# Attention stacks on SyncE's queue as plain float32, the first head's straight from SBUF; layer 1's last modulations beside its attention

## The chip, the cores and the metric

The kernel runs on one core of one Trainium2 chip. A core has a matrix engine (TensorE, PE in the profile), a vector engine (VectorE, DVE), an activation engine (ScalarE, ACT), GpSimd (POOL) and SyncE (SP), which only issues DMAs. Each engine works through its own list of instructions in order and waits at semaphores for the others. DMAs are issued by SP and by POOL here; they move data between DRAM, the large memory, and SBUF, the on-chip one of 128 partitions. Matmuls write to PSUM. The metric is the device time of one execution in microseconds.

## The reference, cut to what matters

Two layers work on 512 latent and 256 context tokens of 1024 features. In each layer a normalized and modulated input is projected, four mixers run side by side (an S5 state-space scan, a gated recurrence, differential attention, gated linear attention), each is projected and multiplied with a gate, and their sum is projected into the residual; then a feed-forward net with a small convolution follows. The second layer computes latent tokens only at its output.

```python
# modulation: six chunks of 1024 per layer from the conditioning vector
m = jax.nn.silu(cond) @ w[:, :n_chunks * D_MODEL] + b[:n_chunks * D_MODEL]
...
# differential attention: 4 heads, 2 components of 32 features each
s = jnp.einsum('bhcqd,bhckd->bhcqk', q, k).astype(F32) * (DA_HEAD ** -0.5)
p = jax.nn.softmax(s, axis=-1)
w = p[:, :, 0] - lam * p[:, :, 1]
return jnp.einsum('bhqk,bhkv->bhqv', w.astype(v.dtype), v)
```

The sixth chunk of the modulation is the gate with which the feed-forward net's result goes into the residual.

## The kernel before, in words

[...] To keep precision each operand is split into a high part and the rest (`hi`, `lo`), and a product is three matmuls: hi x hi, lo x hi, hi x lo. Weights come from DRAM by `load_raw` (line 183, on SP's queue) into a ring of four buffers `wraw`; ScalarE casts the high part (`whi`, line 193), VectorE subtracts (`wlo`, line 194), and the matmuls of `proj` (line 220) use both. Features lie on the partitions, tokens along the free dimension.

The attention's scores are made another way. Each of the eight (head, component) groups has 32 features, a quarter of the partitions. So the four products hi/lo by hi/lo of a group are stacked along the partitions into one matmul of 128: the queries' tile `dstq` holds rows hi, hi, lo, lo and the keys' tile `dstk` hi, lo, hi, lo, 32 partitions each. `da_prep` (line 845) normalizes and rotates queries and keys of two heads and splits them into `dhi` and `dlo`, and writes both into a DRAM buffer `dstk{layer}{half}{q or k}` (line 863). `da_stack` (line 867) reads the tiles of one head back from there, with each row block read twice: four DMAs for queries (line 876) and two for keys (line 879). All of these DMAs are issued by GpSimd; the tiles `dstq` and `dstk` have the type float32r, the DRAM buffer float32.

`da_mix` prepares the first two heads, stacks head 0, prepares the other two, and then runs through the heads: at the start of head h it asks for the stacks of head h+1, then makes scores (lines 925 to 928), the softmax and the products with the values of each tile of 128 queries. Tiles `dstq` and `dstk` come from a pool of ten buffers, shared with others, so that the stacks of a head wait for those of the head before last to be free.

The order of the instructions on each engine is written out by a planner ahead of the run. It takes the instructions by priority (the program's order, and `first()` and `mixer()` put the mixers ahead) as soon as its own estimate of the times says that their inputs and buffers are there. The first scores are tied behind the last matmul of a fixed number of merges (`lead`, `DA_LEAD`). Beside the attention, PE works on gates and branch projections (`merge_branch`), in layer 1 also on six gates made early.

The modulations are made by `ada` (matmuls of line 282, closing ones of line 269): a pair of column blocks at a time, with two loads of 512 KB on SP's queue whose `wraw` buffers the matmuls read directly. `LAST` are the last four pairs, the sixth chunk. They run in the feed-forward net of their own layer: two steps ahead of it (`FILL2`, in the gap of the normalization), the others between its blocks (`side`).

Of the kernel before, what the change touches and what calls it, by code (L numbers as in the profile page):

```python
# [22 lines left out]
T = NLAT + NCTX  # L23
DEPTH = 2
# [50 lines left out]
def f32(ap):  # L75
    return ap.bitcast(F32)
# [3 lines left out]
def backbone(ctx, tc, xT, cT, w_ada, w_in, w_v, w_ga, w_branch, w_out, w_up, w_down, vec,  # L80
             s5_b, s5_c, s5_d, w_glu, lru_w, gla_wa2, consts, masks, rope, cmask, out, dbg=None):
    nc = tc.nc
# [21 lines left out]
    def H(name, shape=None, dt=F32):  # L104
        return gp_.tile(shape or [P, 512], dt, tag="h", name=name, bufs=6)
# [41 lines left out]
    def V(l, name):  # L147
        o, n = VOFF[name]
        return vt[l][:, o:o + n]
# [9 lines left out]
    for l in range(DEPTH):  # L159
        t = cpool.tile([P, 3, 4], F32, name=f"lru_s{l}")  # L160
# [142 lines left out]
    FIRST = range(KT)  # L303
    REST = range(KT, 20)
    LAST = range(20, 24)
# [113 lines left out]
    for l in range(DEPTH):  # L419
# [3 lines left out]
            k=dp.tile([2, P, 240], F32, name=f"s5k{l}"),  # L423
# [421 lines left out]
    def da_prep(l, i, qk, sg, qgs, rp):  # L845

        v = nc.vector
        stk = []
        for which, z, s_, gain in (("q", qk[0], sg, qgs), ("k", qk[1], [LAT, CTX], V(l, 'k_g'))):
            n = s_[-1][1]  # L850
            r = group_rstd(z, C('bo32'), DA_HEAD, s_, "d" + which)
            v.tensor_scalar_mul(z[:, :n], z[:, :n], gain)
            sw = G("dsw")
            v.stream_shuffle(sw[:, :NLAT], z[:, :NLAT], [j ^ 8 for j in range(32)])
            v.tensor_mul(z[:, :NLAT], z[:, :NLAT], rp[0])
            v.tensor_mul(sw[:, :NLAT], sw[:, :NLAT], rp[1])
            v.tensor_add(z[:, :NLAT], z[:, :NLAT], sw[:, :NLAT])
            v.tensor_mul(z[:, :n], z[:, :n], r[:, :n])
            hi, lo = G("dhi", dt=F32R), G("dlo", dt=F32R)
            split(z, hi, lo, 0, n)  # L860
            dd = dp.tile([4, 2, 32, T], F32, name=f"dstk{l}{i}{which}")
            for p_, t_ in enumerate((hi, lo)):
                nc.gpsimd.dma_start(dd[:, p_, :, :n], f32(t_[:, :n]))
            stk.append(dd)
        return stk

    def da_stack(stk, hh, sg):
        res = []
        for dd, n, which in ((stk[0], sg[-1][1], "q"), (stk[1], T, "k")):
            ts = []  # L870
            for c in range(2):
                g = hh * 2 + c
                t = Z("dst" + which, dt=F32R)
                if which == "q":
                    for p_ in range(2):
                        nc.gpsimd.dma_start(t[64 * p_:64 * p_ + 64, :n],
                                            dd[g, p_][:, :n].unsqueeze(0).broadcast_to([2, 32, n]))
                else:
                    nc.gpsimd.dma_start(t[:, :n],
                                        dd[g].rearrange("h r n -> (h r) n")[:, :n].unsqueeze(0).broadcast_to([2, 64, n]))  # L880
                ts.append(t)
            res.append(ts)
        return res

    def da_mix(l, qks, vt_, lat_only):
        v = nc.vector
        e = NLAT if lat_only else T
        sg = [LAT] if lat_only else [LAT, CTX]
# [20 lines left out]
        yield  # L909
        res = []  # L910
        stks = [da_prep(l, 0, qks[0], sg, qgs, rp)]
        st = da_stack(stks[0], 0, sg)
        stks.append(da_prep(l, 1, qks[1], sg, qgs, rp))
        o = None
        lead = yield
# [69 lines left out]
        for hd in range(4):  # L985
            cur = st
            if hd < 3:
                st = da_stack(stks[(hd + 1) // 2], (hd + 1) % 2, sg)
# [188 lines left out]
    def drain(gen):  # L1177
        while True:
            try:
                next(gen)  # L1180
            except StopIteration as s:
                return s.value
# [11 lines left out]
    def chain(*gens):  # L1194
        for g in gens:
            yield from g

    def zipgen(main, fill, n):
        for _ in main:
            for _ in range(n):  # L1200
                next(fill, None)
            yield
# [18 lines left out]
    def gate(l, b, m, h, sg, t):  # L1221
        w = load_split(w_in[l, 18 + b * 8 + m])
        proj("ps_g", w, h, sg, lambda ps, a, b: nc.scalar.activation(t[:, a:b], ps, AF.Tanh, scale=0.5))
        return t

    def merge_branch(l, b, h, y, acc, sg, first, gates=()):

        v = nc.vector
        wb = None
        for m in range(KT):  # L1230
            if m % 4 == 0:
                wb = load_split(w_branch[l, b, m // 4], nk=2, cols=512)
            if m < len(gates):
                t = gates[m]
            else:
                t = gate(l, b, m, h, sg, gp_.tile([P, T], F32, tag="gate", name="gate", bufs=2))
            if first:
                acc.append(X("acc"))

            def use(ps, a, b):  # L1240
                dst = acc[m] if first else t
                v.scalar_tensor_tensor(dst[:, a:b], t[:, a:b], 1.0, ps, op0=ALU.add, op1=ALU.mult)  # L1242
                if not first:
                    v.tensor_add(acc[m][:, a:b], acc[m][:, a:b], t[:, a:b])
            proj("ps_p", wb, y, sg, use, c0=(m % 4) * P)
            yield
# [63 lines left out]
    for l in range(DEPTH):  # L1310
        lat_only = l == DEPTH - 1
        sg = [LAT] if lat_only else sg_all
        if l == 0:
            with first() if NF else nullcontext():
                h = norm_mod(l, x, V(l, 'norm1'), 0, 1, [(0, T)], (marks[M0], marks[M1]))
        else:
            with first():
                h = norm_mod(l, x, V(l, 'norm1'), 0, 1, sg_all)
        for k in range(KT):
            dump(f"h{l}_{k}", f32(h[k][0]))  # L1320
        if l == 0:
            xd = xT
        else:
            xd = dp.tile([KT, P, T], F32, name="x_spill")
            for k in range(KT):
                nc.gpsimd.dma_start(xd[k][:, :NLAT], x[k][:, :NLAT])
        rest = ada(l, REST) if l == 0 else iter(())
        acc = []
        if l == 0:
            with tc.high_priority(offset=-PREP_LAST):  # L1330
                for _ in range(PREP_EARLY):
                    next(prep)
        li = lru_in(l, h, sg_all, sg)
        if l == 0:
            with tc.high_priority(offset=-PREP_LAST), tc.issue_after(li[2]):
                drain(prep)
        yl = mixer(lru_mix(l, *li[:2], lat_only))
        ud = s5_u(l, h, sg_all)
        gi = gla_in(l, h, sg_all, sg)
        yg = mixer(gla_mix(l, *gi, lat_only))  # L1340
        ys = mixer(s5_mix(l, ud, lat_only))
        drain(zipgen(merge_branch(l, 1, h, yl, acc, sg, True), rest, 1))
        qk0 = da_qk(l, h, 0, sg_all, sg)
        dv = proj_tok(l, 0, h, "dv")
        qk1 = da_qk(l, h, 1, sg_all, sg)
        dm = da_mix(l, (qk0, qk1), dv, lat_only)
        with first():
            next(dm)
            next(dm)
        mb = merge_branch(l, 3, h, yg, acc, sg, False)  # L1350
        for _ in range(DA_LEAD[l]):
            next(mb)
            next(rest, None)
        yd_ = mixer(sent(dm, lastp[0]))
        drain(zipgen(mb, rest, 1))
        drain(zipgen(merge_branch(l, 0, h, ys, acc, sg, False), rest, 1))
        early = [gate(l, 2, m, h, sg, H("gate")) for m in range(EARLY if lat_only else 0)]
        drain(zipgen(merge_branch(l, 2, h, yd_, acc, sg, False, early), rest, 1))
        drain(rest)
        for nm, yy in (("yb", yl), ("yd", yg), ("yc", yd_), ("ya", ys)):  # L1360
            for i in range(2):
                dump(f"{nm}{l}_{i}", f32(yy[i][0]))
        e = sg[-1][1]
        x = [X(f"x{k}") for k in range(KT)]
        with after():
            for k in range(KT):
                nc.sync.dma_start(x[k][:, :e], xd[k][:, :e])
        parts = [(0, 256), (256, NLAT)] if lat_only else sg_all
        out_proj(l, acc, x, sg, parts)
        for k in range(KT):  # L1370
            dump(f"xm{l}_{k}", x[k])
        with first():
            h = norm_mod(l, x, V(l, 'norm2'), 3, 4, parts)
        nxt = chain(ada(l, LAST), *([ada(l + 1, FIRST), ada(l + 1, REST)] if l + 1 < DEPTH else []))
        for _ in range(FILL2):
            next(nxt)
        if l + 1 < DEPTH:
            with tc.high_priority(offset=-PREP_LAST):
                drain(s5_prep(l + 1))
        def side():  # L1380
            for _ in range(2):
                next(nxt, None)
        ffn(l, h, x, sg, side)
        drain(nxt)
        for k in range(KT):
            dump(f"xo{l}_{k}", x[k])
# [128 lines left out]
```

## Time and profile before

| | |
|---|---|
| median of 3 runs | 2375.47 us (2369.54 to 2381.79) |
| the profiled execution | 2370.35 us, its span 2368.6 us |
| PE busy | 2262.0 us, 96% of the span |
| VectorE, ScalarE busy | 1327.7 us (56%), 914.5 us (39%) |
| mean granted clock of TensorE | 0.976 |
| DMA on SP's queue | 222.13 MB |
| DMA on GpSimd's queue | 33.70 MB |

A share of busy time is an average over the whole span. Where PE stands still is seen in the list of waits and in the chain of work that ended last, and what happens at such a place in the timeline of the engines around it. [...]

### The profile page before, as it was taken

What the parts mean: (1) busy time and instruction counts of PE and PEld (TensorE: products, weight loads), DVE (VectorE), ACT (ScalarE), POOL (GpSimd) and SP (SyncE); (2) the same over time, 40 slices, a digit from 0 to 9 for tenths busy, and PEclk for the clock granted to TensorE, in tenths of its full rate; (3) what the DMA queues carried; (4) which work ended last, traced back from release to release, by engine and by line L of the source; (5) the groups of instructions that cost most, each with busy time, mean ns of one, the idle gap of its engine ahead of it and who ended that gap; (6) DMA issues with size and microseconds to landing.
All of it is one profiled execution on the core that took longest, in us unless ns stands there. A gap on an engine that the chain in (4) does not pass through costs nothing. (4 is left out here: it accounts for less than half of the span.)

```text
span 2368.6 us, 34594 instructions
## 1 busy us (share of the span) xinstructions
PE 2262.0 (96%) x13848; PEld 1895.3 (80%) x13848; DVE 1327.7 (56%) x2831; ACT 914.5 (39%) x1428; POOL 101.3 (4%) x164
## 2 busy tenths in 40 slices
PE   5999999699999999999999999999979899999999
PEld 3788788588888788888888887878858688888887
DVE  7886663576674585343334347465557655444444
ACT  6735133445432333132121226633355643323332
POOL 0010000200000010000000000000021000000000
PEclk8999999799999999999999999999989999999999
DMA  7243234554223244233232332224454333333332
GB/s 268 89 140 124 72 114 130 124 129 107 83 98 116 72 128 134 89 111 102 91 101 87 116 121 74 83 87 120 124 130 116 76 101 104 120 111 89 90 111 75
DMA packets 128176, 258.04 MB, mean 109 GB/s; under 512 B 52816, under 2 KB 61072, under 8 KB 128016
## 3 DMA queue, kind: packets, MB, share of 16 engines
q1 hardware_dynamic: 85136, 222.13, 29.4%
q0 software_dynamic: 42880, 33.70, 6.1%
q8 instruction: 109, 1.79, 0.3%
q14 instruction: 51, 0.42, 0.1%
HBM read 230.78 MB, written 24.87 MB: 108 GB/s over the span
## 5 line engine op out<-in xcount | busy, mean ns | idle before, releaser
L194 DVE TENSOR_TENSOR wlo<-wraw,whi 128x1024 fp32r<-128x1024 f32 (+2 forms) x284 | 325.7, 1148 | 327.9 <-ACT whi L193 308.2
L193 ACT CAST whi<-wraw 128x1024 fp32r<-128x1024 f32 (+2 forms) x284 | 280.6, 989 | 579.6 <-PE ps_fd L220 211.6
L220 PE MATMUL ps_g<-hi,whi 128*128 128x512 f32 (+1 forms) x768 | 278.8, 363 | 2.8 <-DVE gate L1242 2.8
L220 PE MATMUL ps_g<-hi,wlo 128*128 128x512 f32 (+1 forms) x768 | 276.5, 360 | 0.0
L220 PE MATMUL ps_g<-lo,whi 128*128 128x512 f32 (+1 forms) x768 | 275.9, 359 | 0.0
L220 PE MATMUL ps_fg<-hi,whi 128*128 128x512 f32 (+1 forms) x544 | 195.0, 360 | 8.0 <-ACT hi L366 7.4
L220 PE MATMUL ps_fg<-hi,wlo 128*128 128x512 f32 (+1 forms) x544 | 191.6, 353 | 0.0
L220 PE MATMUL ps_fg<-lo,whi 128*128 128x512 f32 (+1 forms) x544 | 188.4, 354 | 0.0
L220 PE MATMUL ps_fa<-hi,whi 128*128 128x512 f32 (+1 forms) x528 | 187.5, 355 | 0.0
L220 PE MATMUL ps_fa<-lo,whi 128*128 128x512 f32 (+1 forms) x528 | 187.3, 355 | 0.0
L220 PE MATMUL ps_fd<-uhi,whi 128*128 128x512 f32 (+1 forms) x528 | 187.2, 355 | 0.0
L220 PE MATMUL ps_fd<-ulo,whi 128*128 128x512 f32 (+1 forms) x528 | 187.0, 355 | 0.0
L220 PE MATMUL ps_fa<-hi,wlo 128*128 128x512 f32 (+1 forms) x528 | 186.9, 354 | 0.0
L220 PE MATMUL ps_fd<-uhi,wlo 128*128 128x512 f32 (+1 forms) x528 | 186.0, 354 | 0.0
L220 PEld LDWEIGHTS ps_g<-hi,whi 128*128 128x128 f32 x768 | 145.9, 190 | 29.6 <-issue 5.5
L220 PEld LDWEIGHTS ps_g<-hi,wlo 128*128 128x128 f32 x768 | 145.6, 190 | 23.2 <-issue 2.4
L220 PEld LDWEIGHTS ps_g<-lo,whi 128*128 128x128 f32 x768 | 146.0, 190 | 21.9 <-issue 1.6
L1292 DVE SCALAR_TENSOR_TENSOR x<-ps_fd,mod,x 128x512 f32<-128x512 f32 (+1 forms) x96 | 63.2, 661 | 149.6 <-PE ps_fd L220 149.4
L220 PEld LDWEIGHTS ps_fg<-hi,whi 128*128 128x128 f32 x544 | 104.5, 192 | 31.5 <-ACT hi L366 8.9
L220 PEld LDWEIGHTS ps_fg<-hi,wlo 128*128 128x128 f32 x544 | 105.1, 193 | 13.9 <-issue 1.0
L1285 DVE TENSOR_TENSOR fy<-ps_fa,fy 128x512 f32<-128x512 f32 x66 | 39.8, 603 | 132.3 <-PE ps_fa L220 132.3
L220 PEld LDWEIGHTS ps_fd<-uhi,whi 128*128 128x128 f32 x528 | 99.8, 189 | 15.7 <-DVE fy L1285 1.6
(471 smaller groups left out, 4743.9 us busy)
## 6 DMA issues: line engine op xcount, KB each, us to landing
wraw<-in_w_ada_dram SPq DMA_DIRECT2D x96, 512.0 KB, 3.5
wraw<-in_w_in_dram SPq DMA_DIRECT2D x92, 512.0 KB, 3.9
wraw<-in_w_up_dram SPq DMA_DIRECT2D x88, 512.0 KB, 3.5
wraw<-in_w_down_dram SPq DMA_DIRECT2D x32, 384.0 KB, 3.2
wraw<-in_w_down_dram SPq DMA_DIRECT2D x32, 320.0 KB, 3.0
wraw<-in_w_branch_dram SPq DMA_DIRECT2D x16, 512.0 KB, 5.0
wraw<-in_w_out_dram SPq DMA_DIRECT2D x16, 512.0 KB, 3.6
x<-in_xT_dram SPq DMA_DIRECT2D x16, 384.0 KB, 4.7
```

The source lines that it names most:

```text
L193: nc.scalar.copy(hi, raw)
L194: nc.vector.tensor_sub(lo, raw, f32(hi))
L220: lastp[0] = nc.tensor.matmul(ps[:, c - a:d - a], wt[:, k, c0:c0 + P], act[k][x_][:, c:d], start=i == 0, stop=i == 3 * n - 1).ins
L1285: proj("ps_fa", wa, h, sg, lambda ps, a, b: v.tensor_mul(y[:, a:b], ps, y[:, a:b]), late=f < LATE2)
L1292: v.scalar_tensor_tensor(x[m][:, a:b], ps, mods[l][:, 5 * KT + m, i:i + 1], x[m][:, a:b], op0=ALU.mult, op1=ALU.add)
```

## The change

The attention's writes to DRAM and reads from there are issued by SP, and the tiles are seen as plain float32, so that source and destination have one type. The stacks of head 0 no longer go through DRAM: each of their row blocks is copied from `dhi` or `dlo` in SBUF to the tile in SBUF, four copies of 32 partitions a tile, sixteen in all. The writes to DRAM of the first two heads stay, as head 1 is read from there. In layer 1 the last four pairs of the modulation are asked for in the program ahead of the early gates, beside the attention; nothing is left there to be made in the feed-forward net of layer 1.

```diff
             for p_, t_ in enumerate((hi, lo)):
-                nc.gpsimd.dma_start(dd[:, p_, :, :n], f32(t_[:, :n]))
-            stk.append(dd)
+                nc.sync.dma_start(dd[:, p_, :, :n], f32(t_[:, :n]))
+            stk.append((dd, hi, lo))
         return stk
 
-    def da_stack(stk, hh, sg):
+    def da_stack(stk, hh, sg, direct=False):
+
         res = []
-        for dd, n, which in ((stk[0], sg[-1][1], "q"), (stk[1], T, "k")):
+        for (dd, hi, lo), n, which in ((stk[0], sg[-1][1], "q"), (stk[1], T, "k")):
             ts = []
             for c in range(2):
                 g = hh * 2 + c
                 t = Z("dst" + which, dt=F32R)
-                if which == "q":
+                if direct:
+                    for r in range(4):
+                        p_ = r // 2 if which == "q" else r % 2
+                        nc.sync.dma_start(f32(t[32 * r:32 * r + 32, :n]), f32((hi, lo)[p_][32 * g:32 * g + 32, :n]))
+                elif which == "q":
                     for p_ in range(2):
-                        nc.gpsimd.dma_start(t[64 * p_:64 * p_ + 64, :n],
-                                            dd[g, p_][:, :n].unsqueeze(0).broadcast_to([2, 32, n]))
+                        nc.sync.dma_start(f32(t[64 * p_:64 * p_ + 64, :n]),
+                                          dd[g, p_][:, :n].unsqueeze(0).broadcast_to([2, 32, n]))
                 else:
-                    nc.gpsimd.dma_start(t[:, :n],
-                                        dd[g].rearrange("h r n -> (h r) n")[:, :n].unsqueeze(0).broadcast_to([2, 64, n]))
+                    nc.sync.dma_start(f32(t[:, :n]),
+                                      dd[g].rearrange("h r n -> (h r) n")[:, :n].unsqueeze(0).broadcast_to([2, 64, n]))
                 ts.append(t)
...
         stks = [da_prep(l, 0, qks[0], sg, qgs, rp)]
-        st = da_stack(stks[0], 0, sg)
+        st = da_stack(stks[0], 0, sg, True)
...
         drain(zipgen(merge_branch(l, 0, h, ys, acc, sg, False), rest, 1))
+        if lat_only:
+            drain(ada(l, LAST))
         early = [gate(l, 2, m, h, sg, H("gate")) for m in range(EARLY if lat_only else 0)]
...
-        nxt = chain(ada(l, LAST), *([ada(l + 1, FIRST), ada(l + 1, REST)] if l + 1 < DEPTH else []))
+        nxt = iter(()) if lat_only else chain(ada(l, LAST), ada(l + 1, FIRST), ada(l + 1, REST))
         for _ in range(FILL2):
-            next(nxt)
+            next(nxt, None)
```

## Rows read from the trace of the kernel before

**Rows 1.** The page: busy us, share of the span and instructions.
```profile
PE 2262.0 (96%) x13848; PEld 1895.3 (80%) x13848; DVE 1327.7 (56%) x2831; ACT 914.5 (39%) x1428; POOL 101.3 (4%) x164
```
**Rows 2.** Waits of PE: who waited for whom, us in total, times, longest.
```profile
PE ps_s L925 <- DMA dstq<-dstk00q: 21.0, 1, 21.0
...
PE ps_s L925 <- DMA dstq<-dstk10q: 14.0, 1, 14.0
```
**Rows 3.** Timeline of PE, first scores of both layers: start, us, what [idle before].
```profile
457.46 0.77 PE L925 MATMUL ps_s<-dstk,dstq 128*128 128x512 f32 x1 [20.99 <-DMA dstq<-dstk00q]
...
1762.58 0.77 PE L925 MATMUL ps_s<-dstk,dstq 128*128 128x512 f32 x1 [14.05 <-DMA dstq<-dstk10q]
```
**Rows 4.** Windows: us, busy us by engine, granted clock, DMA share, GB/s.
```profile
460.00:470.00 10.00, 10.00 (x52) 7.29 (x45) 8.16 (x25) 6.02 (x8) 1.53 (x2) 0.87 0.80 219
...
1765.00:1770.00 5.00, 5.00 (x19) 3.76 (x18) 4.41 (x6) 0.84 (x2) 0.67 (x1) 0.86 0.61 107
```
**Rows 5.** Timeline of VectorE: the low part of the first keys, both layers.
```profile
427.26 0.95 DVE L200 TENSOR_TENSOR dlo<-dzk,dhi 128x768 fp32r<-128x768 f32 x1
...
1734.48 0.95 DVE L200 TENSOR_TENSOR dlo<-dzk,dhi 128x768 fp32r<-128x768 f32 x1
```
**Rows 6.** Timeline of POOL: DMA issues of the stacks.
```profile
431.74 0.72 POOL L863 DMA_DIRECT2D dstk00k<-dhi  x1
...
443.89 1.62 POOL L879 DMA_DIRECT2D dstk<-dstk00k  x2 [10.73 <-DMA dstk00k<-dlo]
...
504.20 2.63 POOL L876 DMA_DIRECT2D dstq<-dstk01q  x4 [31.15 <-PE ps_ada L269]
...
550.56 2.68 POOL L876 DMA_DIRECT2D dstq<-dstk01q  x4 [34.26 <-PE ps_s L932]
...
1801.52 2.63 POOL L876 DMA_DIRECT2D dstq<-dstk11q  x4 [20.71 <-PE ps_s L928]
...
1833.90 2.60 POOL L876 DMA_DIRECT2D dstq<-dstk11q  x4 [24.32 <-PE ps_s L928]
```
**Rows 7.** Timeline of SP: one weight load near layer 1's first scores.
```profile
1749.44 0.33 SPq L183 DMA_DIRECT2D wraw<-in_w_in_dram  x1
```
**Rows 8.** DMA issues: line's tiles, queue, count, KB each, median us to landing.
```profile
s5ph<-cph POOLq DMA_DIRECT2D x4, 384.0 KB, 3.1
...
s5u<-us SPq DMA_DIRECT2D x4, 384.0 KB, 2.4
...
dstk00q<-dhi POOLq DMA_DIRECT2D x1, 384.0 KB, 8.9
dstk00q<-dlo POOLq DMA_DIRECT2D x1, 384.0 KB, 12.8
```
**Rows 9.** Tiles dstq (first line) and dstk (second): their DMAs.
```profile
DMA to landing us min/median/max: 5.3/9.4/15.1
...
DMA to landing us min/median/max: 11.5/14.8/18.2
```
**Rows 10.** Chain that ended last, start of layer 1's feed-forward net: start, us, what.
```profile
1988.89 5.12 DMA wraw<-in_w_up_dram
...
2002.40 1.00 PE ps_ada L282 x16
...
2005.72 0.34 PE ps_ada L269 x4
```
**Rows 11.** Windows: the end of layer 1's attention.
```profile
1866.00:1901.00 35.00, 21.88 (x156) 17.09 (x156) 21.31 (x31) 19.83 (x47) 0.00 (x0) 0.78 0.05 15
```
**Rows 12.** Timeline of ScalarE at the start of layer 1's feed-forward net.
```profile
1994.08 1.04 ACT L193 CAST whi<-wraw 128x1024 fp32r<-128x1024 f32 x1 [2.85 <-DMA wraw<-in_w_up_dram]
1995.03 1.30 ACT L366 ACTIVATE hi<-full,mod 128x256 fp32r<-128x256 f32 x3
```
**Rows 13.** Windows: the stretch of layer 0's wait.
```profile
441.00:457.00 16.00, 0.00 (x0) 0.00 (x0) 0.94 (x3) 0.84 (x1) 3.57 (x5) 0.50 0.49 91
```
**Rows 14.** Page: SP's DMA queue, packets, MB, share of 16 engines' span.
```profile
q1 hardware_dynamic: 85136, 222.13, 29.4%
```

## The prediction

> **What bounds the kernel now.** I read the page's busy shares first. TensorE (PE) is busy 96% of the span [rows 1], so only two things can shorten the kernel: time in which PE stands still, and work that leaves PE. So the next view is the list of what PE waited for. Its first and third entries are one kind of wait: the scores of attention (ps_s) wait for the stacked queries dstq, 21.0 us once in layer 0 and 14.0 us once in layer 1 [rows 2]. Each is one single wait, and it stands ahead of the first scores of the first head: PE stops at 457.46 - 20.99 = 436.47 us and at 1762.58 - 14.05 = 1748.53 us [rows 3]. No other head waits for a stack. After such a stop PE also runs slowly for a while: the granted clock is 0.87 over 460 to 470 us and 0.86 over 1765 to 1770 us [rows 4], which is the lower of the two levels (0.50) until about 462.6 and 1766.4 us, so 5.1 us at half speed lose 2.6 us and 3.8 us lose 1.9 us.
>
> Why the stack is late: the low part of the keys is finished by VectorE at 427.26 + 0.95 = 428.2 us, in layer 1 at 1735.4 us [rows 5]. GpSimd issues the keys' first write into DRAM only at 431.74 us, because its queue is in order and stood behind the reads of the queries, and the reads back at 443.89 us [rows 6]. So of the 29.3 us from 428.2 to 457.5, 3.5 go to the order in the queue, 12.2 to the way out to DRAM and 13.6 to the way back.
>
> **The change, part by part.** All sums are made against the profiled execution: 2370.35 us, of which 2368.6 are span.
>
> *First head, layer 0.* Removed: GpSimd's order and the way through DRAM. Added on SyncE (SP), for queries and for keys alike: two writes (still needed by the second head) and eight copies from SBUF to SBUF, ten issues of 0.33 us [rows 7], 3.3 us. Queries are split before keys, so their ten go out ahead. Those of the keys are issued by 428.2 + 3.3 = 431.5 us. How fast they land is not in the trace: no transfer of SP goes from SBUF to SBUF, and none has these shapes. From below: 2.4 us, a 384 KB store of SP; from above: 12.8 us, the slowest of the first two writes of this stack on GpSimd's queue [rows 8]. That is 433.9 to 444.3 us, against PE's stop at 436.47, so a wait of 0 to 7.8 us remains, and the gain is 21.0 to 13.2 us. I take 8.9 us, the landing of the first such write [rows 8], since these two writes go ahead of the copies in the same queue: 440.4 us, a wait of 3.9 us, **gain 17.1 us**. I count nothing for the clock here, as PE still stands; if the wait goes altogether, 2.6 us more.
>
> *First head, layer 1.* 1735.4 + 3.3 + 8.9 = 1747.6 us, before PE's stop at 1748.53: **gain 14.0 us and 1.9 us** of half clock. With 12.8 us it would be 1751.5, a wait of 3.0 us, gain 11.0. What is late next is the end of the fixed lead of merge matmuls behind which the first scores are put; PE is full there.
>
> [...]
>
> *The later heads.* Their stacks still go through DRAM, now on SP: 16 writes, 24 reads for queries and 12 for keys, beside 32 direct copies: 84 issues more for SP, where GpSimd loses 64. SP's queue is in order too, and it carries the weights. A stack transfer that waits (for its tile, until the head before last has had its scores) holds the weight loads behind it; a weight load that waits for a buffer holds the stacks behind it. PE waits for neither before: stacks of heads 1 to 3 do not appear among its waits [rows 2]. A head takes 46.4 us in layer 0 (504.20 to 550.56) and 32.4 us in layer 1 (1801.52 to 1833.90) [rows 6], and its six transfers land in 5.3 to 15.1 us (queries) and 11.5 to 18.2 us (keys), overlapping [rows 9]. From below nothing is lost. From above, if the six go one behind another at their median, it is 4 x 9.4 + 2 x 14.8 = 67.2 us a head; the second and third head after the first have just one head's time for it, so (67.2 - 46.4) x 2 + (67.2 - 32.4) x 2 = 111 us. I take **8 us lost**, a quarter of a head in layer 1, near the lower end, because what the trace shows (waits of heads 1 to 3: none) is nearer to that.
>
> *Modulations beside the attention.* Four pairs of columns, each 16 matmuls of 1.00 us and four closing ones of 0.34 us [rows 10]: 5.4 us leave the FFN. The first pair ran in the gap before the FFN, where PE had nothing else, so 3 x 1.34 = **4.0 us** come off the path. In attention they are covered by the tail: from 1866 to 1901 us PE is busy for 21.88 of 35 us at a clock of 0.78 [rows 11], while ScalarE and VectorE finish the last tiles. 13.1 us idle take 5.4 us of matmuls. Without that cover (if they run earlier, while PE is full) they push other fill work into the same tail, so the cover holds either way; if they delay scores in the tail instead, the gain is 0. Their eight loads of weights go on SP ahead of the last gates'.
>
> *Start of the FFN.* The chain has 5.12 us of waiting for a load of w_up at 1988.89 us [rows 10], whose buffer the moved loads had held. ScalarE sat on that load: its cast starts at 1994.08 and the first modulated tile only at 1995.03 us [rows 12], though ScalarE had been idle for the 2.85 us before that cast. With the load early the cast ends by 1992.3: **gain 2.7 us** (0 to 5.1: the modulated tiles themselves may be what is late).
>
> Sum: 17.1 + 14.0 + 1.9 + 4.0 + 2.7 - 8 = 31.7 us, 2370.35 - 31.7 = 2338.7 us. The profiled run is 5.1 us below the median of the runs shown (2375.47; 2369.54 to 2381.79); I add half of it: **2341 us**.
>
> **Rivals.** *A, slower: the later heads' stacks hold up the scores.* Mechanism: on one queue the six transfers of a head line up and end late. For it: writes of 384 KB into the stack land in 8.9 and 12.8 us where a 384 KB write of another shape, same queue, takes 3.1 us [rows 8], so this shape is slow by itself; from 441 to 457 us, with nothing else running, five such transfers keep 0.49 of the DMA engines busy and move 91 GB/s [rows 13]. Against it: at the shortest landings a head needs 4 x 5.3 + 2 x 11.5 = 44.2 us [rows 9], nothing in layer 0 and 11.8 x 2 = 24 us in layer 1: 2357 us. At the medians it is 2341 + 111 - 8 = 2444 us. It decides from where a head's six take T = 50 us: 2 (T - 46.4) + 2 (T - 32.4) = 42 us, the forecast's gain against the median and its 8 us.
>
> [...]
>
> *B, about the same: the first head's copies stand behind weight loads.* SP issues a weight load at 1749.44 us, as soon as a buffer is free [rows 7]. The order in the queue is written ahead by the planner's estimates. If the keys' copies stand behind that load, they land at 1749.8 + 3.3 + 8.9 = 1762.0 us and layer 1 gains nothing: 2341 + 15.9 = 2357 us. If layer 0 has the same, 17.1 us more: 2374 us, and the change does not do what it says.
>
> **How the numbers follow.** The forecast has 0.62, its own range 2318 to 2356 us (2320 is 21.0 + 2.6 + 14.0 + 1.9 + 5.4 + 5.1 off the profiled run). B has 0.20, 2357 to 2374. A has 0.18, 2357 to 2444. What a measurement here can tell from no change is 0.5%, 12 us: 2363.6 to 2387.4. Faster: 0.62 and about half of B, 0.71. Same: the rest of B and a little of A, 0.14. Slower: the most of A, 0.15. The range is 2318 to 2386: below it 0.04, above it 0.15.
>
> **What would show it.** Right: PE's waits for stacks sum to under 8 us; the first scores start near 441 and within 2 us of their predecessors in layer 1; no ps_ada matmul in the last FFN; the first ps_fg some 3 us sooner after the last ps_wo. Wrong by A: new waits of ps_s for dstk or dstq at heads 1 to 3, or of whi for wraw in attention. Wrong by B: the copies' issue on SP later than the split of the keys by more than 4 us, and the old first waits.

## The result and the profile after

The changed kernel takes 2408.61 us (median; 2407.25 to 2411.4) where the kernel before took 2373.85 in the same runs: the ratio is 1.0144 [1.0114, 1.0174], slower by 34.8 us. The forecast was 2341 us, in a range of 2318 to 2386. The profiled execution after has 2407.3 us, of which 2405.4 are span, 36.8 more than before; the mean granted clock went from 0.976 to 0.969.

The list of what PE waited for, after (who for whom; us in total, times, longest), answers to [rows 2]:

```profile
PE ps_ada L282 <- DMA wraw<-in_w_ada_dram: 41.3, 3, 23.5
PE ps_s L930 <- ACT dp L943: 16.3, 2, 14.8
PE ps_s L930 <- DMA dstk<-dhi: 10.1, 1, 10.1
PE ps_ada L282 <- ACT gate L1228: 9.0, 1, 9.0
PE ps_g L220 <- ACT whi L193: 7.2, 2, 6.9
PE ps_s L930 <- DMA dstk<-dlo: 6.4, 1, 6.4
```

Of the first line 17.5 us are a wait at the start of the program, which every kernel here has in this or another name; the other 23.8 are new. The two waits that the change was about did shrink, 21.0 to 10.1 and 14.0 to 6.4 us. The other four lines are new or grown (the wait for dp was 3.3 us before), and none of them names a stack: they name weights (wraw, whi), the softmax (dp) and a gate. What is new in them sums to 23.8 + 13.0 + 9.0 + 7.2 = 53.0 us, and the two stack waits are 18.5 us shorter: 34.5 of the 36.8 us.

Where they come from is in the chain of waits (start, us, what), after, from the end of layer 0's first stacks on:

```profile
438.17 6.32 DMA dstk<-dhi
444.53 0.77 PE ps_s L930
...
450.85 7.64 DMA wraw<-in_w_ada_dram
458.49 17.88 DMA dstk01q<-dlo
...
480.52 20.42 DMA wraw<-in_w_in_dram
...
536.03 22.50 DMA wraw<-in_w_in_dram
```

Loads of w_in of 512 KB take 20.42 and 22.50 us from issue to landing. The same load before, in the page's list of DMA issues (queue, count, KB each, median us to landing):

```profile
wraw<-in_w_in_dram SPq DMA_DIRECT2D x92, 512.0 KB, 3.9
```

What stands ahead of the load of 536.03 is in SP's timeline after (start, us, what):

```profile
519.82 2.66 SPq L881 DMA_DIRECT2D dstq<-dstk01q  x4
522.58 13.35 SPq L884 DMA_DIRECT2D dstk<-dstk01k  x2
536.03 7.62 SPq L183 DMA_DIRECT2D wraw<-in_w_in_dram  x1
```

Six stack reads of a later head, and right behind them the weight load. SP itself is stuck in the issues, 13.35 us for two where one issue before, of a weight load, took 0.33 [rows 7]. One alone took 12.82, the largest of that line in the groups of tile dstk (ns min/median/max, first and last start):

```profile
L884 SPq DMA_DIRECT2D dstk<-dstk01k x4: 482/4382/12823, 522.6 to 585.2; - x4
```

The windows of that stretch, and of one in which PE stands (us, busy us by engine, granted clock, DMA share, GB/s), after:

```profile
525.00:530.00 5.00, 5.00 (x29) 4.15 (x27) 2.59 (x4) 0.76 (x2) 0.00 (x0) 1.00 0.13 47
530.00:535.00 5.00, 5.00 (x37) 4.20 (x36) 2.92 (x5) 3.83 (x9) 0.00 (x0) 1.00 0.14 53
535.00:540.00 5.00, 5.00 (x40) 3.69 (x39) 3.71 (x6) 2.77 (x6) 0.00 (x0) 1.00 0.14 52
460.00:480.00 20.00, 5.23 (x25) 4.40 (x24) 5.07 (x16) 4.25 (x7) 0.00 (x0) 0.65 0.28 93
```

Read the last two columns. A DMA share of 0.13 to 0.14 is 2.1 to 2.2 of 16 engines on average, moving some 50 GB/s, while six transfers and soon a weight load are waiting to be moved. Before, five such transfers on GpSimd's queue kept 0.49 busy and moved 91 GB/s [rows 13]. The last line is what such queueing does elsewhere: PE busy for 5.23 of 20 us, at a clock of 0.65. The share is a mean over all 16; which of them are busy the windows do not show.

The wait for dp is the same queue seen from the other end. ScalarE's timeline, after (start, us, what [idle before]):

```profile
468.88 0.90 ACT L943 ACTIVATE dp<-ps_s,d_nm 128x768 f32<-128x768 f32 x1 [7.50 <-DMA dstk01q<-dhi]
...
476.39 0.90 ACT L943 ACTIVATE dp<-ps_s,d_nm 128x768 f32<-128x768 f32 x1 [6.51 <-DMA dstk01q<-dlo]
```

The softmax's tile dp shares its buffers with dhi and dlo, and it had to wait until the writes of these into DRAM, issued late and slow (17.88 us in the chain), had landed.

Layer 1 has the same at the end of its attention. SP's timeline and PE's, after:

```profile
1853.54 6.72 SPq L881 DMA_DIRECT2D dstq<-dstk11q  x4
1860.35 10.79 SPq L884 DMA_DIRECT2D dstk<-dstk11k  x2
1871.24 10.93 SPq L183 DMA_DIRECT2D wraw<-in_w_ada_dram  x4
```
```profile
1894.18 2.26 PE L282 MATMUL ps_ada<-wraw,cs 128*32 128x256 f32 x16 [23.48 <-DMA wraw<-in_w_ada_dram]
```

The moved modulations' loads stand behind the last head's stacks, and PE waits 23.48 us for them. That looks like a fault of the move; whether it is was left to an experiment.

The feed-forward net of layer 1 did start sooner. PE's timeline after, its first matmul and the last one ahead of it:

```profile
2032.62 0.28 PE L220 MATMUL ps_wo<-hi,wlo 128*128 128x256 f32 x1
...
2037.12 0.58 PE L220 MATMUL ps_fg<-hi,whi 128*128 128x256 f32 x1 [0.61 <-ACT hi L366]
```

The gap is 4.2 us (2037.12 - 2032.90); before it was 7.3 (1988.26 to 1995.59 in PE's timeline).

### The profile page after: what moved, and what is told of

The parts are those of the page before. It is cut to its first block, busy times and chain, and to the rows that moved or that the text cites. A ratio compares the mean times of both kernels' runs of the same rounds, so it can differ in the third digit from the quotient of the medians.

```text
span 2405.4 us, 34618 instructions
## 1 busy us (share of the span) xinstructions
PE 2272.3 (94%) x13848; PEld 1899.4 (79%) x13848; DVE 1327.9 (55%) x2831; ACT 914.3 (38%) x1428; POOL 55.6 (2%) x100
## 4 chain that ended last, share of the span: by engine, by line
PE 87%; DMA 5%; DVE 4%; ACT 2%; SPq 1%; issue 1%; ACTq 0%; DVEq 0%
PE ps_g L220 17%; PE ps_fg L220 13%; PE ps_fd L220 13%; PE ps_fa L220 13%; PE ps_wo L220 5%; PE ps_p L220 4%; DMA wraw<-in_w_in_dram 2%; PE ps_ada L282 2%; PE ps_vdv L246 1%; PE ps_vgv L246 1%; PE ps_u L220 1%; PE ps_lx L220 1%; PE ps_gg L220 1%; PE ps_ly L220 1%; PE ps_k L220 1%; PE ps_o L974 1%
## 5 line engine op out<-in xcount | busy, mean ns | idle before, releaser
L220 PEld LDWEIGHTS ps_fg<-lo,whi 128*128 128x128 f32 x544 | 101.6, 190 | 13.8 <-DVE lo L367 0.8
```

The lines of the kernel that those rows point to most:

```text
L220: lastp[0] = nc.tensor.matmul(ps[:, c - a:d - a], wt[:, k, c0:c0 + P], act[k][x_][:, c:d], start=i == 0, stop=i == 3 * n - 1).ins
```

## The experiments

The cut of a transfer means here how its source and destination are divided: the outermost size is the count of the first of the nested steps in which a DMA goes through one side. A key read takes 2 times 64 rows, so its outermost size is 2; a write into the DRAM buffer takes 4 blocks of 32 rows, so its is 4. Both are called narrow below, and pieces of 32 or 128 rows, where the rows themselves are outermost, wide.

Theory: the narrow cut of the stack transfers is what costs, and SP's queue turns it into late weights. Rivals: SP's queue is the wrong place for them whatever their cut; or the moved modulations do it.

### The modulations alone, and the rest without them

e1: the kernel before with the modulations moved. e2: the changed kernel with them put back.

```diff
+        if lat_only:
+            drain(ada(l, LAST))
         early = [gate(l, 2, m, h, sg, H("gate")) for m in range(EARLY if lat_only else 0)]
...
-        nxt = chain(ada(l, LAST), *([ada(l + 1, FIRST), ada(l + 1, REST)] if l + 1 < DEPTH else []))
+        nxt = iter(()) if lat_only else chain(ada(l, LAST), ada(l + 1, FIRST), ada(l + 1, REST))
```

> The kernel before with only layer 1's last modulations moved beside its attention. Between the kernels before and after, the stretch from the last projection matmul of layer 1 to the end got 7.8 us shorter (start of the last ps_wo 1987.9 and 2032.4 us, spans 2368.6 and 2405.4 us). Theory W (the move is a gain, and was spoiled in the changed kernel only by late weight loads): the 7.8 us stay, the attention does not get longer, 2366 us. Rival (the eight loads and 5.4 us of matmuls delay the scores by themselves): no change or up to 10 us slower, 2374 to 2384 us.

> The changed kernel with only the modulations put back into the feed-forward net. Theory W (weight loads queue behind the stacks of the later heads): PE's wait of 23.5 us for a modulation's weights in layer 1 goes, the 7.8 us of the feed-forward net come back, and the gates' weights are late instead by a few us: 2408.6 - 23.5 + 7.8 + about 3 = 2396 us, still slower than before. Rival (the move itself is what made the change slow): 2345 us or less.

e1: 2369.43 us against 2373.27, ratio 0.9987 [0.9975, 0.9999], 3.8 us less by the medians and 3.1 by the ratio; 2366 us had been expected. e2: 2409.32 us, ratio 1.0152 [1.013, 1.0175]: the whole loss is still there, so the modulations are not its cause. The number expected of e2 was missed. In the place where PE waited 23.48 us for the modulations' weights, e2's chain of waits has another load behind the same stacks:

```profile
1873.69 22.77 DMA wraw<-in_w_in_dram
```

What comes next on SP's queue is late there; the moved loads only happened to be it. In the changed kernel the move is worth nothing that shows (2408.61 and 2409.32), and this is the likely reason.

### Only the first head's copies on SP

e4: the kernel before with head 0 copied from SBUF by SP; writes and later heads stay on GpSimd.

```diff
+                if direct:
+                    for r in range(4):
+                        p_ = r // 2 if which == "q" else r % 2
+                        nc.sync.dma_start(f32(t[32 * r:32 * r + 32, :n]), f32((hi, lo)[p_][32 * g:32 * g + 32, :n]))
+                elif which == "q":
...
-        st = da_stack(stks[0], 0, sg)
+        st = da_stack(stks[0], 0, sg, True)
```

> The kernel before with only the first head's stacks copied straight from SBUF by SP; the writes to DRAM and the later heads' stacks stay on GpSimd, the modulations stay. Theory W: the first-head waits of 21.0 and 14.0 us shrink to under 5 us each and nothing else gets late, as SP carries no transfer with a small outer dimension: 2374 - 27 = 2347 us. Rival (the copies of 32 rows behind weight loads on SP are late themselves, or the buffers dhi and dlo are held longer): no gain, 2370 us or more.

2350.7 us, ratio 0.9913 [0.9893, 0.9933]: 22.6 us less, near what was expected. In the edits e2 differs from e4 by nothing but the issuer of the writes and of the later heads' reads, and the type of these reads: 2409.32 - 2350.7 = **58.6 us** in the same runs. That is the price of the part called "later heads". The first head's wait did not go altogether; PE's waits in e4:

```profile
PE ps_s L929 <- DMA dstk<-dlo: 15.1, 2, 10.9
```

Under 5 us each had been expected; the longer one is 10.9.

### The cut of the transfers

e3: the changed kernel with the same bytes in another cut. The DRAM buffer has its hi/lo index outermost, so that a write is one piece of 128 rows; each tile is read in four pieces of 32 rows instead of two (queries) or one (keys) of twofold repeated rows. All on SP, with more DMAs than before.

```diff
-            dd = dp.tile([4, 2, 32, T], F32, name=f"dstk{l}{i}{which}")
+            dd = dp.tile([2, 4, 32, T], F32, name=f"dstk{l}{i}{which}")
...
-                nc.sync.dma_start(dd[:, p_, :, :n], f32(t_[:, :n]))
+                nc.sync.dma_start(dd[p_].rearrange("g r n -> (g r) n")[:, :n], f32(t_[:, :n]))
...
+                for r in range(4):
+                    p_ = r // 2 if which == "q" else r % 2
+                    src = f32((hi, lo)[p_][32 * g:32 * g + 32, :n]) if direct else dd[p_, g][:, :n]
+                    nc.sync.dma_start(f32(t[32 * r:32 * r + 32, :n]), src)
```

> The changed kernel with another cut of the same transfers, all still on SP's queue: the DRAM buffer is ordered so that a write is 128 rows of one piece on both sides, and each stack is read in four pieces of 32 rows, as the direct copies are, instead of reads with a doubled outer dimension of 2 and writes with one of 4. Same bytes, more issues: 96 reads for 36. Theory W (the reads with an outer size of 2 run on two DMA engines: from 520 to 540 us of the changed kernel 0.13 of 16 engines are busy, 2.1, and move 44 GB/s): DMA is spread, weights land in time, PE waits less than 10 us in all for stacks and weights in attention: 2374 - 17 - 14 - 8 = 2335 us. Rival Q (SP's one in-order queue is the cause: stacks that wait for tiles hold weight loads back): more issues make it no better, 2400 us or more.

**2327.44 us, ratio 0.9814 [0.9797, 0.9832]**: faster than the kernel before by 45.8 us and than the changed one by 81. SP's timeline and the windows of e3, for the stretch that answers to 519 to 540 above:

```profile
485.19 3.58 SPq L878 DMA_DIRECT2D dstq<-dstk01q  x8
488.86 3.62 SPq L878 DMA_DIRECT2D dstk<-dstk01k  x8
492.58 0.37 SPq L183 DMA_DIRECT2D wraw<-in_w_in_dram  x1
```
```profile
460.00:480.00 20.00, 20.00 (x144) 16.77 (x144) 17.97 (x57) 10.78 (x24) 0.00 (x0) 1.00 0.33 106
...
485.00:496.00 11.00, 11.00 (x79) 9.42 (x79) 7.97 (x34) 3.21 (x10) 0.00 (x0) 1.00 0.62 191
```

Sixteen issues in 7.2 us where six took 16.0; 191 GB/s, with a weight load among them, where it was 50; and PE is full in both windows. The time is 8 us below the 2335 that had been expected. No stack is left in PE's list of waits. That SP is the wrong queue is refuted: in e3 all stack transfers are on it.

e5: only the reads are cut anew, the buffer and its writes (outermost size 4) stay.

```diff
+                    src = f32((hi, lo)[p_][32 * g:32 * g + 32, :n]) if direct else dd[g, p_][:, :n]
```

> The changed kernel with only the reads of the stacks cut into pieces of 32 rows; the sixteen writes to DRAM keep their outer dimension of 4 (they write into four blocks of 32 rows that don't adjoin). [...] Rival (writes and reads matter alike): 2365 us or more.

2348.68 us, ratio 0.9892 [0.9873, 0.991]. With ratios on the 2374 us of before, the reads' cut is worth (1.0144 - 0.9892) x 2374 = 60 us and the writes', with the reads already wide, (0.9892 - 0.9814) x 2374 = 19 us, which was missed: 2337 us and 5 to 15 for the writes had been the author's estimate, from a number of engines for them that no run shows. What the writes cost is in e5's waits, the changed kernel's two first-head waits, nearly unchanged:

```profile
PE ps_s L923 <- DMA dstk<-dhi: 9.7, 1, 9.7
...
PE ps_s L923 <- DMA dstk<-dlo: 5.4, 1, 5.4
```

So with narrow writes the copies of head 0 are late, and with wide ones (e3) they are not. Whether it matters that the writes go ahead of the copies on the same queue is not shown: in e4 they go on GpSimd's, and the two waits are 15.1 us in sum, as here (9.7 + 5.4). The window of e4's first wait has a DMA share of 1.07, GpSimd's transfers and SP's at once:

```profile
436.00:448.00 12.00, 1.14 (x5) 0.85 (x4) 5.84 (x19) 6.40 (x8) 0.72 (x1) 0.62 1.07 165
```

Which transfer holds up which copy is open, and so is whether it is the writes' outermost size of 4 or that their four blocks do not adjoin in DRAM.

e8 asks whether it is the outermost size or the repeated rows: e3, but the keys of the later heads are read in two pieces of 64 rows, each from a source of outermost size 2, nothing repeated.

```diff
+                    if not direct and which == "k":
+                        if p_ == 0:
+                            nc.sync.dma_start(f32(t[32 * r:32 * r + 64, :n]), dd[:, g][:, :, :n])
+                        continue
```

> The wide cut, with one thing put back: the keys of the later heads are read in two pieces of 64 rows a tile, each from a source of outer size 2 by 32 rows, with nothing read twice by one DMA. Theory W (the outer size of 2 is the cause): their 0.79 MB a head run on two engines at 44 GB/s, 18 us, about 0.13 of 16 engines busy while they run; weights behind them are late by up to 18 us, which the prefetch covers in part: 2335 to 2360 us. Rival (the doubled reading, a stride of zero, is the cause): as e3, 2327 us, and 0.3 or more of the engines busy.

2341.1 us, ratio 0.9858 [0.9841, 0.9875], above e3 by 13.7 us, or 10.4 by the ratios. Two windows of e8:

```profile
494.00:497.00 3.00, 3.00 (x20) 2.50 (x18) 1.76 (x1) 0.76 (x2) 0.00 (x0) 1.00 0.13 45
512.00:516.00 4.00, 4.00 (x32) 3.75 (x30) 1.76 (x1) 2.75 (x7) 0.00 (x0) 1.00 0.13 52
```

The first stands right behind the issue of four such reads (490.51 to 493.57 us in SP's timeline of e8). The share is the same 0.13 as before: the outermost size does it, not the repetition. The second stands 18 us behind that issue, while SP is in the issues of two weight loads (504.05 us, 15.60 us long). That weight loads behind such reads move at this share too is seen in the changed kernel: from 525 to 530 us 79 packets carry 0.24 MB at a share of 13.0%, some 3 KB each, the rows of the keys; from 556 to 560 us 59 packets, 7 of them under 512 B, carry 0.21 MB at the same 13.0% and 52 GB/s, some 4 KB each without the small ones, the rows of the weights. So what is left of a weight load behind the reads moves at the same small share. Why, and whether on the same engines, is not shown.

### The queue, the type and the straight path, at the better cut

e6: the kernel before, all on GpSimd and into float32r tiles, with only the cut of e3.

```diff
-                nc.gpsimd.dma_start(dd[:, p_, :, :n], f32(t_[:, :n]))
+                nc.gpsimd.dma_start(dd[p_].rearrange("g r n -> (g r) n")[:, :n], f32(t_[:, :n]))
...
+                for r in range(4):
+                    p_ = r // 2 if which == "q" else r % 2
+                    nc.gpsimd.dma_start(t[32 * r:32 * r + 32, :n], dd[p_, g][:, :n])
```

> The kernel before, all on GpSimd's queue and with its type change from float32 to float32r, with only the cut of the transfers changed: writes of 128 rows in one piece, reads of 32 rows. Theory W: both hops land in about 4 us where they took 9 to 16, and the first-head waits fall from 21.0 and 14.0 us to under 8 and 4 us: 2373 - 23 = 2350 us. Rival (GpSimd's queue or the type change is what is slow): the waits stay within 4 us of before, 2370 us or more, more issues of 0.7 us on GpSimd included.

2334.87 us, ratio 0.9833 [0.9815, 0.9851], better than expected. Neither wait of [rows 2] is left, without any of the edits of the change. Not all of that is the quicker stack: in layer 0 the last reads of head 0's keys have landed at 439.6 us, 3 us after PE stopped before, and the planner now puts other work ahead of the first scores, which start at 452.99 us. The DMA issues of e6, which answer to [rows 8]:

```profile
dstq<-dstk00q POOLq DMA_DIRECT2D x16, 96.0 KB, 2.4
dstk<-dstk00k POOLq DMA_DIRECT2D x16, 96.0 KB, 3.3
...
dstk00q<-dhi POOLq DMA_DIRECT2D x1, 384.0 KB, 2.7
dstk00q<-dlo POOLq DMA_DIRECT2D x1, 384.0 KB, 3.1
```

The writes of 8.9 and 12.8 us land in 2.7 and 3.1, on the same queue, with the same bytes.

e7: e3 without the straight path, head 0 through DRAM as the others. e9: e3 with the modulations put back into the feed-forward net.

```diff
-        st = da_stack(stks[0], 0, sg, True)
+        st = da_stack(stks[0], 0, sg)
```

> The wide cut on SP, with the first head's stacks through DRAM again. Theory W: two hops of 4 to 5 us on SP are nearly as good as one: keys written by 429.5, landed 434, read back by 441 to 443 us where PE runs out at about 436: a wait of 5 to 7 us in layer 0, under 3 us in layer 1, 2327 + 8 = 2335 us. Rival (the way straight from SBUF is what made e3 fast): the old waits of 21 and 14 us return by more than half, 2345 us or more.

```diff
-        if lat_only:
-            drain(ada(l, LAST))
...
-        nxt = iter(()) if lat_only else chain(ada(l, LAST), ada(l + 1, FIRST), ada(l + 1, REST))
+        nxt = chain(ada(l, LAST), *([ada(l + 1, FIRST), ada(l + 1, REST)] if l + 1 < DEPTH else []))
```

> The wide cut on SP with the first head straight from SBUF, but the modulations of layer 1 put back into its feed-forward net. In e1 the move of the modulations gave 3 us beside stacks on GpSimd. Theory W: with weights in time it gives the 4.0 + 2.7 us of the prediction, so without it 2327 + 7 = 2334 us. Rival (the attention of layer 1 pays back what the feed-forward net gains): 2327 to 2330 us.

e7: 2328.22 us, ratio 0.9803 [0.9788, 0.9817], the same as e3 and 7 us below the 2335 expected. Its first scores start at 436.35 us with no wait for a stack, and the straight path is worth nothing that shows once the way through DRAM is quick. e9: 2333.69 us, ratio 0.9833 [0.9818, 0.9848]; the modulations are worth some 6 us when weights come in time. And e9 against e6, 0.9833 both: at this cut SP against GpSimd, float32 against float32r and the straight path together make no difference that shows. At the narrow cut there is one: e2 and e4 differ by issuer and type, and 58.6 us lie between them.

### A shorter lead

e10: e3 with `DA_LEAD = (2, 2)` instead of (2, 3), so that layer 1's first scores stand behind one merge less.

```diff
-DA_LEAD = (2, 3)
+DA_LEAD = (2, 2)
```

> The wide cut with one merge fewer ahead of layer 1's first scores (DA_LEAD 2 and 2 for 2 and 3), as the stacks are there earlier. If the end of layer 1's attention is what leaves PE idle at its end, the scores start about 7 us earlier and the idle time of the tail shrinks by up to that: 2320 to 2327 us. If the stacks are not there yet, or the fill work lacks later: 2327 to 2335 us.

2327.71 us, ratio 0.9806 [0.9789, 0.9822]: no change against e3, the hoped-for gain missed. The first scores of layer 1 did not move: they start at 1724.34 us, in e3 at 1723.39. So the lead is not what sets their start here, and the run does not say what an earlier start would give.

## Why the prediction was wrong

**The step that failed is "the later heads".** It took 8 us out of bounds of 0 to 111, with the reason that PE waited for none of these stacks before. They measure 58.6 us (e2 against e4). The reason was no reason: on GpSimd's queue, which carried nothing urgent behind them, a slow transfer of a later head made nobody late. On SP's queue the weights stand behind it. What mattered was what is next in the queue that they move to, and the prediction named it in words and priced it at a quarter of a head. The sum with the measured sizes, on the 2373.3 us of before in those runs: -22.6 (first head, e4) + 58.6 - 0.7 (modulations, e2 against the changed kernel) = +35.3, 2408.6 us. It comes out at the time measured because each term is a difference of two of these kernels; it says how the loss divides and proves nothing more.

**Rival A** had the place and the sign, and its 2357 to 2444 hold the result. Its mechanism was half right: in heads 1 to 3 the scores never wait for a stack out of DRAM. It is the weights and the softmax's buffers that are late. The second sign named for A, casts that wait for weights in attention, came; the kernel before has none of them in layer 0's attention, and after there are three (ScalarE's waits, 436 to 680 us):

```profile
ACT whi L193 <- DMA wraw<-in_w_in_dram: 21.1, 3, 10.2
```

The weight loads were the larger part of the new waits (23.8, 9.0 and 7.2 us, against 13.0 more for dp; the gate of the 9.0 stands behind a cast that waited for its weights). The evidence was there: five transfers with nothing else running kept only 0.49 of the 16 engines busy, 7.8 on average [rows 13], and A got 0.18. That row should have weighed more than a list of waits from a kernel in which nothing urgent stood behind the stacks.

**The first head.** Forecast was a gain of 17.1 + 14.0 + 1.9 = 33.0 us, measured 22.6 alone (e4) and waits shorter by 10.9 and 7.6 in the changed kernel. From the split of the keys (427.74) to the first scores (444.53) it took 16.8 us, not 3.3 + 8.9 = 12.2. The issues were mis-sized: SP's timeline after, some of the keys' copies:

```profile
430.66 2.37 SPq L863 DMA_DIRECT2D dstk00k<-dlo  x1
433.08 1.39 SPq L878 DMA_DIRECT2D dstk<-dlo  x1
...
435.91 2.22 SPq L878 DMA_DIRECT2D dstk<-dlo  x1
438.17 1.63 SPq L878 DMA_DIRECT2D dstk<-dhi  x1
```

Ten issues go out in some 14 us (429.41 to 443.42), not 3.3. In e3 the same ten take 5.9 us (430.37 to 436.26), most of the copies 0.58 to 0.60 each, so the 0.33 of a weight load was too little for them at either cut, and the rest came with the narrow transfers. Why the stacks were late before was also told wrong: not GpSimd's order and not the way through DRAM as such, but the cut. e6 has both and its stack has landed by 439.6 us instead of 458.1; e7 has the way through DRAM and no wait.

**Rival B** did not happen: the keys' copies go out from 430.04 us, 2.3 us after the split, and in layer 1 no weight load stands between the split and the copies.

**The modulations and the start of the feed-forward net** were right as steps, 4.0 + 2.7 = 6.7 us: from the last ps_wo on, after gains 7.8 us (PE's last ps_wo matmul is 44.6 us later than before, the end 36.8), and e9 against e10, which took the time of e3 in the same runs as e9, gives 6.0. The cover in attention is what failed: in the changed kernel, where the loads were behind the stacks, and in part in e1. There 7.5 us are gained from the last ps_wo on, and PE has a wait in layer 1's attention that the kernel before has not:

```profile
PE ps_ada L282 <- DMA wraw<-in_w_ada_dram: 4.7, 2, 4.4
```

That leaves 2.8 us, close to the 3.1 to 3.8 measured.

Open: how much of the 58.6 us is the low rate of the reads (a DMA share of 0.13) and how much the order in the queue, as no run separates the two at the narrow cut.

## What to carry to other kernels

Before a transfer is moved to another queue, ask what stands behind it there, and measure what rate its cut gets there (reads of outermost size 2 gave 45 to 53 GB/s here): a list of waits from the old queue says nothing about the new one. When a DMA of some hundred KB lands in 9 to 15 us where another of the same size takes 3, and the DMA share is at 0.13 or some other small fraction with transfers in flight, change the cut first; here that alone brought 39.7 us (e6), with the queue, the type and a way around DRAM together worth nothing that shows beside it. An edit that shortens a wait by going around a slow transfer can be worth something alone (22.6 us in e4) and nothing once the transfer is mended (e7).

## What the runs showed of the hardware that was not expected

- More and smaller DMAs were quicker: sixteen reads of 96 KB instead of six of 192 and 384 KB, 7.2 us of issues instead of 16.0, and 191 GB/s, a weight load included, instead of 50.
- An issue on SP does not always take 0.33 us: 12.82 us were seen for one read of 384 KB behind five others.
- Weight loads behind reads of outermost size 2 moved at a DMA share of 0.13, as the reads did (13.0% and 52 GB/s at 556 to 560 us of the changed kernel), and loads behind such reads landed 20.42, 22.50 and 22.77 us after their issue instead of 3.9 (the chains of the changed kernel and of e2).
- Reads into float32r tiles by GpSimd are not slow as such: 96 KB land in 2.4 to 3.8 us (median of a group, e6).
